# A hybrid SSD and GLA trunk layer: part two begins with the last block's u, held in SBUF

## Chip, cores and metric

The kernel runs on one core of a Trainium2 chip. The metric is the time of one execution on the device, in microseconds; lower is better. The engines are named as in the profile: PE is TensorE (PEld its weight loads), DVE VectorE, ACT ScalarE, POOL GpSimd, SP SyncE, which issues most DMAs.

## What is computed

One layer over 2048 tokens and 16 meta tokens ahead of them, model width 1024, all in float32:

```
u = rmsnorm(h)
z, xbc, dt, q, k, v, g, a_lr, merge_g = split(u @ w_in)
y_ssd = rmsnorm_groups(ssd(conv(xbc), dt) * silu(z))        # 4 groups, state carried along the tokens
y_gla = rmsnorm_heads(gla(q, k, v, a_lr)) * silu(g)         # 4 heads, chunks of 64 tokens
merged = sum over b of sigmoid(merge_g[b]) * (y_b @ w_branch[b])
out = final_rmsnorm(h + merged @ w_out)
```

## The kernel before

Every float32 product is made of three products of split operands: an operand is split into a rounded high part (ACT copies it to fp32r) and the rest (DVE or POOL subtracts), and `accum` (L183-187) issues high by high, high by low and low by high. These are L185, L186 and L187 in the profile.

**Part one** goes over four blocks of 512 tokens (block 0 has the 16 meta tokens besides). `u` of a block is held split in SBUF, in a pool of two tiles, so that `u` of the last block lies there until part one ends; a copy goes to DRAM. In a block come four groups of the SSD branch and four heads of the GLA branch. Each is a projection (u by weights, `ssd_proj` or `gla_proj`), whose generator yields between its pieces, and a scan (`ssd_scan` or `gla_scan`), a generator that `step()` advances by one piece at each of those yields: the scan of a head runs beside the projection of the next. Behind the last head there is no projection left beside which its scan could run. Weights come through a ring of four tiles `whl` (`load_w`, L158-168). In block 0 a weight of 128 x 512 is read from DRAM, split by ACT (L165) and POOL (L166), and its split form, 512 KB, is saved to DRAM (L181); later blocks read that back and split nothing (L161).

The last `gla_scan` has these steps: L688 to L695 on DVE and ACT (decays), L703 on PE, in bank `pc`, L773 and L724 and L790 on PE in bank `pt`, L781 on DVE, which completes an operand from `pt`; then for each chunk L185 to L187 and L801 on PE into `pc`, L802 on DVE (the state), L804 and L806 on ACT (the chunk's output and its square sum, after which `pc` is free); then `rstd`, L811 on ACT, transposes L816 on PE, L817 on DVE, and the store of y (L820, issued by ACT).

**Part two** computes gates, branch products and the output product by a Strassen-Winograd scheme: a product of 2 x 2 tiles takes seven products P1 to P7 of 12 matmuls of 128 x 512 each, instead of eight. A is the weight (a pair n of weight tiles), B the activations of two blocks. P1 and P2 take the first column of B as it lies (`B11`, `B21`), P3 the other; P4 to P7 take sums of B, which are made beside part one and lie in DRAM. Stages come in the order gate0, branch 0 and 1 of blocks 0 and 1, gate1, branch 0 and 1 of blocks 2 and 3, out. In a `Stage`, `load_b` (L898) and `prep_b` (L903 on ACT, L904 on DVE) load and split an operand of B, `load_a` (L910) loads four 256 KB tiles of A of a pair, `sum_a` (L919 to L922 on POOL, four operations) makes A's sums, `prep_a` splits (L928 on ACT, L929 on DVE), `product` issues the matmuls and copies a result that is needed again (L945). A gate is finished by a sum (L965), tanh (L972) and a store (L1104).

PE's and SP's instructions stand in the order in which the code issues them (`manual_schedule`); for ACT, DVE and POOL a scheduler sets the order, except that SP alone is by hand once the loop of stages has begun. The dictionary `between` says what is issued between the steps of the last scan: loads and splits for P1 and P2 of the pairs 0 and 1 of gate0, and P1 and P2 of pair 0; the products of pair 1 follow, moved up among them. `inputs.close()` gives the memory of u and of the weights to these operands. Behind the scan a table `todo` gives each load and split its place (positions in `order`), and `run(i)` issues what is due.

## Time and profile before

| what | value |
|---|---|
| runs shown | 2332.26, 2326.44, 2332.66 us; median 2332.26 |
| profiled execution | 2329.27 us |
| its span | 2327.3 us |
| mean granted TensorE clock | 0.988 |
| busy: PE, DVE, ACT, POOL | 97%, 67%, 51%, 29% of the span |
| DMA | 518.05 MB, mean 223 GB/s |

The page gives busy time of each engine, the span in 40 slices, and groups of instructions with the idle time ahead of them. The timeline lists instructions by start; the brackets at the end of a row give the idle time of the engine just before it and what ended it. Rows marked SPq or ACTq are issues of DMAs on that engine's queue. The windows cut the span into stretches.

### The profile page before, as it was taken

What the parts mean: (1) busy time and instruction counts of PE and PEld (TensorE: products, weight loads), DVE (VectorE), ACT (ScalarE), POOL (GpSimd) and SP (SyncE); (2) the same over time, 40 slices, a digit from 0 to 9 for tenths busy, and PEclk for the clock granted to TensorE, in tenths of its full rate; (3) what the DMA queues carried; (4) which work ended last, traced back from release to release, by engine and by line L of the source; (5) the groups of instructions that cost most, each with busy time, mean ns of one, the idle gap of its engine ahead of it and who ended that gap; (6) DMA issues with size and microseconds to landing.
All of it is one profiled execution on the core that took longest, in us unless ns stands there. A gap on an engine that the chain in (4) does not pass through costs nothing. (4 is left out here: it accounts for less than half of the span.)

```text
span 2327.3 us, 36519 instructions
## 1 busy us (share of the span) xinstructions
PE 2247.1 (97%) x12641; PEld 1956.3 (84%) x12641; DVE 1550.3 (67%) x2895; ACT 1184.8 (51%) x2758; POOL 684.6 (29%) x681
## 2 busy tenths in 40 slices
PE   7899999999999999999999999889999999999998
PEld 7899888888888989898988898768888888888776
DVE  5676766676675666566568555654588954788766
ACT  4666655465544455544465443554554545554443
POOL 3344433122221122212122100037324264324331
PEclk9999999999999999999999999989999999999999
DMA  8766865767785666786677655457577866687743
GB/s 302 230 204 208 292 228 205 223 199 237 244 284 181 214 213 217 255 270 215 194 230 214 206 168 162 145 178 247 186 255 268 305 227 216 231 286 259 243 145 122
DMA packets 301545, 518.05 MB, mean 223 GB/s; under 512 B 27696, under 2 KB 143664, under 8 KB 301360
## 3 DMA queue, kind: packets, MB, share of 16 engines
q1 hardware_dynamic: 200400, 402.84, 53.0%
q10 hardware_dynamic: 100960, 112.88, 14.1%
q8 instruction: 99, 1.62, 0.3%
q14 instruction: 86, 0.70, 0.1%
HBM read 368.42 MB, written 147.19 MB: 222 GB/s over the span
## 5 line engine op out<-in xcount | busy, mean ns | idle before, releaser
L185 PE MATMUL pj<-u,whl 128*128 128x512 f32 (+1 forms) x1184 | 449.0, 379 | 14.6 <-ACT acc L475 6.7
L187 PE MATMUL pj<-u,whl 128*128 128x512 f32 (+1 forms) x1184 | 433.5, 366 | 1.4 <-POOL whl L166 0.8
L186 PE MATMUL pj<-u,whl 128*128 128x512 f32 (+1 forms) x1184 | 432.0, 365 | 0.0
L185 PE MATMUL pj<-whl,u 128*128 128x256 f32 (+1 forms) x992 | 289.0, 291 | 2.4 <-ACT u L298 1.5
L187 PE MATMUL pj<-whl,u 128*128 128x256 f32 (+1 forms) x992 | 282.4, 285 | 1.6 <-DVE u L300 1.6
L186 PE MATMUL pj<-whl,u 128*128 128x256 f32 (+1 forms) x992 | 282.2, 284 | 1.0 <-POOL whl L166 1.0
L185 PEld LDWEIGHTS pj<-u,whl 128*128 128x128 f32 x1184 | 226.8, 192 | 53.7 <-ACT acc L475 7.7
L185 PE MATMUL pj<-b,a 128*128 128x512 f32 x640 | 254.0, 397 | 13.8 <-ACT sn L945 7.6
L187 PEld LDWEIGHTS pj<-u,whl 128*128 128x128 f32 x1184 | 226.0, 191 | 38.0 <-POOL whl L166 1.9
L186 PEld LDWEIGHTS pj<-u,whl 128*128 128x128 f32 x1184 | 227.0, 192 | 33.6
L187 PE MATMUL pj<-b,a 128*128 128x512 f32 x640 | 252.2, 394 | 0.0
L186 PE MATMUL pj<-b,a 128*128 128x512 f32 x640 | 251.0, 392 | 0.0
L185 PEld LDWEIGHTS pj<-whl,u 128*128 128x128 f32 x992 | 189.7, 191 | 4.0 <-ACT u L298 1.8
L187 PEld LDWEIGHTS pj<-whl,u 128*128 128x128 f32 x992 | 189.6, 191 | 2.3 <-DVE u L300 2.3
L80 POOL TENSOR_TENSOR wr<-wr 128x256 f32<-128x256 f32 x80 | 66.3, 829 | 425.0 <-DMA wr<-u 174.7
L186 PEld LDWEIGHTS pj<-whl,u 128*128 128x128 f32 x992 | 189.9, 191 | 1.6 <-POOL whl L166 1.2
L166 POOL TENSOR_TENSOR whl<-wr,whl 128x512 fp32r<-128x512 f32 (+1 forms) x100 | 134.7, 1355 | 187.4 <-ACT whl L165 151.5
L904 DVE TENSOR_TENSOR b<-br,b 128x512 fp32r<-128x512 f32 x196 | 154.9, 808 | 44.7 <-ACT b L903 43.5
L919 POOL TENSOR_TENSOR as<-ar,ar 128x512 f32<-128x512 f32 x40 | 60.0, 1499 | 411.3 <-DMA ar<-in_w_br 197.3
L479 DVE SCALAR_TENSOR_TENSOR acc<-cin,hcw,acc 128x512 f32<-128x512 f32 (+1 forms) x192 | 154.4, 804 | 30.9 <-ACT acc L475 29.8
L929 DVE TENSOR_TENSOR a<-ar,a 128x512 fp32r<-128x512 f32 x160 | 126.3, 797 | 67.2 <-ACT a L928 64.4
L903 ACT ACTIVATE b<-br 128x512 fp32r<-128x512 f32 x196 | 119.4, 626 | 99.0 <-DMA br<-br_t 38.6
(274 smaller groups left out, 5068.8 us busy)
## 6 DMA issues: line engine op xcount, KB each, us to landing
whl<-k_s SPq DMA_DIRECT2D x96, 512.0 KB, 4.5
whl<-k_g SPq DMA_DIRECT2D x96, 512.0 KB, 4.2
whl<-k_v SPq DMA_DIRECT2D x48, 512.0 KB, 3.7
whl<-k_z SPq DMA_DIRECT2D x36, 512.0 KB, 3.8
wr<-in_w_feat SPq DMA_DIRECT2D x64, 256.0 KB, 4.5
k_s<-whl SPq DMA_DIRECT2D x32, 512.0 KB, 3.6
cb<-cumd ACTq DMA_DIRECT2D x64, 256.0 KB, 5.8
y<-gg ACTq DMA_DIRECT2D x64, 256.0 KB, 4.5
```

What stands on the lines that cost most here:

```text
L80: nc.gpsimd.tensor_tensor(o, x, y, op=ALU.subtract)
L166: nc.gpsimd.tensor_tensor(hl[:, 1], raw, hl[:, 0].bitcast(F32), op=ALU.subtract)
L185: nc.tensor.matmul(ps, sh, mh, start=first, stop=False, **kw)
L186: nc.tensor.matmul(ps, sh, ml, start=False, stop=False, **kw)
L187: nc.tensor.matmul(ps, sl, mh, start=False, stop=last, **kw)
L479: nc.vector.scalar_tensor_tensor(acc, cin[:, k:k + tt], hcw[:, ti, k:k + 1], acc, op0=ALU.mult, op1=ALU.add)
L903: nc.scalar.activation(t[:, 0], raw, AF.Copy)
L904: nc.vector.tensor_tensor(t[:, 1], raw, t[:, 0].bitcast(F32), op=ALU.subtract)
L919: nc.gpsimd.tensor_tensor(s1, a21, a22, op=ALU.add)
L929: nc.vector.tensor_tensor(t[:, 1], src, t[:, 0].bitcast(F32), op=ALU.subtract)
```

## The change

Four things are changed; the code's lines move by 5 in `accum` and `load_w`, and more behind.

1. `block_of` makes the last block of a pair the first column of B, so P1 and P2 of gate1 read u of block 3. The stages begin with gate1, then gate0, then the branches. The sums of the branches of blocks 2 and 3, which were made beside gate0 and gate1, are made beside gate1 and gate0.
2. In block 0 `load_w` is called for six weights more, one behind each of the first six heads: those of P1 and P2 of gate1's pairs 0, 1 and 2. They are split and saved like the others.
3. In the last block, from its last head but one on, `early_operands` loads and splits the four B sums of P6 (four loads, four splits) and makes the sums of A for P6 of pairs 0 and 1 (six loads, four POOL operations, two splits), into the tile of u that is free by then.
4. Between the last scan's pieces stand six products, P1 and P2 of the pairs 0, 1, 2, with the six weights (read back from DRAM in split form) and u as it lies in SBUF. Behind the scan's last transposes come the two P6. The loads for the rest of gate1 come behind these, in pools that lie where part one's `first` pool lay; `inputs.close()` follows. Then P7, P5, P3 and P4 of pairs 0 and 1, P1 and P2 of pair 3, and the order as before. A has seven buffers (five and two) in place of six.

```diff
+    def block_of(s, t):
+        return 2 * s + 1 - t
     def braw_u(s):
-        return lambda k, t: u_left[2 * s + t][k]
+        return lambda k, t: u_left[block_of(s, t)][k]
...
+    EARLY = [(n, p) for n in range(3) for p in (1, 2)]
+    last_sums = sums["g", nsb - 1][1][1]
+    b6, s2 = [], {}
+    def gate_w(n, p):
+        return f"m{n}_{p}", w_feat[T_GATE + 2 * n, :, (p - 1) * BLK:p * BLK]
+    def early_operands():
+        room = mk(upool, [P, 2, KT * (META + BLK)], F32R, "u").rearrange("p i f -> p (i f)")
+        tiles = [room[:, j * 1024:(j + 1) * 1024].rearrange("p (i c) -> p i c", i=2) for j in range(6)]
+        b6.extend(tiles[:4])
+        for j in range(0, 4, 2):
+            stage = [mk(wpool, [P, BLK], F32, "wr", bufs=NWR) for _ in range(2)]
+            for i in range(2):
+                nc.sync.dma_start(stage[i], last_sums[j + i][:, 0])
+            yield
+            for i in range(2):
+                split(b6[j + i][:, 0], b6[j + i][:, 1], stage[i])
+            yield
+        for n in range(2):
+            raw = [mk(wpool, [P, BLK], F32, "wr", bufs=NWR)]
+            raw += [mk(wk, [P, META + BLK], F32, "acc")[:, :BLK] for _ in range(2)]
+            for dst, i, j in zip(raw, (1, 1, 0), (0, 1, 0)):
+                nc.sync.dma_start(dst, w_feat[T_GATE + 2 * n + i, :, j * BLK:(j + 1) * BLK])
+            yield
+            nc.gpsimd.tensor_tensor(raw[0], raw[0], raw[1], op=ALU.add)
+            nc.gpsimd.tensor_tensor(raw[0], raw[0], raw[2], op=ALU.subtract)
+            yield
+            s2[n] = tiles[4 + n][:, 0], tiles[4 + n][:, 1]
+            split(*s2[n], raw[0])
...
+            if (b, i) == (nblk - 1, SG + GH - 2):
+                begin(early_operands())
...
+            if b == 0 and i < len(EARLY):
+                load_w(*gate_w(*EARLY[i]))
...
-    inputs.close()
...
-        def product(self, n, p, early=False):
+        def product(self, n, p, early=None, place=None):
             key, pool, tag = {1: ("a", pj, "pj"), 6: ("a",) * 3, 5: ("a",) * 3, 3: ("a",) * 3, 2: ("c", pc, "pc"),
                               7: ("b", pt, "pt"), 4: ("b",) * 3}[p]
             if p in (1, 2, 7):
                 self.ps[n, key] = bank(pool, tag)
             ps = self.ps[n, key]
-            a = self.a[n][p]
...
+            if early is None:
+                a = self.a[n][p]
+                parts = [(a[:, 0, j], a[:, 1, j]) for j in range(4)], [self.b[p, j] for j in range(4)]
+                parts = parts[0], [(t[:, 0], t[:, 1]) for t in parts[1]]
+            else:
+                parts = [tuple(t[:, j * P:(j + 1) * P] for t in early) for j in range(4)], self.early_b(p)
+            for j, (aj, bj) in enumerate(zip(*parts)):
+                accum(ps, aj, bj, p in (1, 2, 7) and j == 0, j == 3, skip_group_check=True)
...
+        def early_b(self, p):
+            if p == 6:
+                return [(t[:, 0], t[:, 1]) for t in b6]
+            return [tuple(t[:, j + 4 * (p - 1), :BLK] for t in next_u[nblk - 1]) for j in range(4)]
...
-    stages = []
+    stages = [gate_stage(s) for s in reversed(range(nsb))]
     for s in range(nsb):
-        stages += [gate_stage(s), branch_stage(s, 0), branch_stage(s, 1)]
+        stages += [branch_stage(s, 0), branch_stage(s, 1)]
...
-    NEARLY = 4
-    order[:NEARLY] = [(stages[0], n, p) for n in range(2) for p in (1, 2)]
+    order = [(stages[0], n, p) for p in PS[3:] for n in range(2)] + [(stages[0], 3, 1), (stages[0], 3, 2)] + order[18:]
+    begins = [max(0, k - 8) for k in begins]
...
-    between = {
-        0: [lambda: st.load_a(0), lambda: b_ops(1, (0, 1))],
-        1: [lambda: b_ops(1, (2, 3)), lambda: st.prep_a(0, 1)],
-        2: [lambda: st.load_a(1), lambda: b_ops(2, (0, 1))],
-        3: [lambda: b_ops(2, (2, 3)), lambda: st.prep_a(0, 2)],
-        4: [lambda: st.product(0, 1, True), lambda: st.prep_a(1, 1)],
-        5: [lambda: st.sum_a(0)],
-        6: [lambda: st.product(0, 2), lambda: st.prep_a(1, 2)],
-        7: [lambda: st.sum_a(1)],
-    }
+    ops = {e: load_w(*gate_w(*e)) for e in EARLY[:4]}
     k = 0
-    while running or begun or k in between:
-        for fn in between.get(k, []):
-            fn()
-        if running or begun:
-            step()
+    while running or begun:
+        step()
+        flush_all()
+        if k in (4, 5):
+            ops[EARLY[k]] = load_w(*gate_w(*EARLY[k]))
+        e = {0: 0, 1: 1, 2: 2, 3: 3, 4: 4, 5: 5}.get(k)
+        if e is not None:
+            place = mk(wk, [P, META + BLK], F32, "acc")[:, :BLK] if EARLY[e][1] == 1 else None
+            st.product(*EARLY[e], ops.pop(EARLY[e]), place)
         k += 1
+    assert not ops
+    flush_all()
+    first.close()
+    bpl.update({p: pool2(f"bops{p}", 4, side="right") for p in (7, 5)})
+    rpl = pool2("raws", 1, side="right")
+    apl = [(pool2("aops", 5, side="right"), 5)] * 5
+    opl, spl = pool2("outs", 1, side="right"), pool2("small", 4, side="right")
+    for n in range(2):
+        st.product(n, 6, s2[n])
+    run(-1)
     ordered.close()
-    first.close()
-    bpl.update({p: pool2(f"bops{p}", 4, side="right") for p in (6, 7, 5, 3, 4)})
-    opl, spl = pool2("outs", 1, side="right"), pool2("small", 4, side="right")
-    bt_raws["all"] = opl, "br", 5
+    inputs.close()
+    bpl.update({p: pool2(f"bops{p}", 4) for p in (3, 4, 1, 2, 6)})
+    apl += [(pool2("aops2", 2), 2)] * 2
```

PE, at the end of the last scan. `pt` behind `cst,ot` are the scan's last transposes (L816 before, L821 after), `pc` ahead of them the last product among the scan's steps, `pj` or `pt` behind them the first one after it. Before:

```order
L185 MATMUL pc_17603<-b_2974_17323,a_17440 128x512
L186 MATMUL pc_17603<-b_2974_17323,a_17440 128x512
L187 MATMUL pc_17603<-b_2974_17323,a_17440 128x512
L816 MATMUL pt_17443<-cst,ot_17341 128x128 x4
L816 MATMUL pt_17449<-cst,ot_17341 128x128 x4
L185 MATMUL pj_17367<-b_3006_17500,a_17512 128x512
L185 MATMUL pj_17575<-b_3006_17500,a_17523 128x512
L186 MATMUL pj_17367<-b_3006_17500,a_17512 128x512
```

And after:

```order
L190 MATMUL pc_17492<-u_11363,whl_17490 128x512
L191 MATMUL pc_17492<-u_11363,whl_17490 128x512
L192 MATMUL pc_17492<-u_11363,whl_17490 128x512
L821 MATMUL pt_17507<-cst,ot_17398 128x128 x4
L821 MATMUL pt_17513<-cst,ot_17398 128x128 x4
L190 MATMUL pj_17278<-u_16199 128x512
L191 MATMUL pj_17278<-u_16199 128x512
L192 MATMUL pj_17278<-u_16199 128x512
```

The last product of the scan reads a weight `whl` and u in place of loaded and split operands `a` and `b`; behind the transposes stands P6 with both operands in the second u tile (`u_16199`), and 24 rows on P7 with loaded operands.

ACT, in the middle of the last scan; `a<-ar` and `b<-br` are splits of operands of part two, the rest are the scan's steps. Before:

```order
L928 ACTIVATE a_17232<-ar_17144 128x512
L691 ACTIVATE sq_17018<-sq_17018 128x64x4
L692 ACTIVATE sq_17018<-sq_17018 128x64x4
L928 ACTIVATE a_17326<-ar_17150 128x512
L903 ACTIVATE b_2924_17154<-br_2923_17152 128x512
L804 ACTIVATE ot_17162<-pc_17164 128x256
L903 ACTIVATE b_2926_17159<-br_2925_17157 128x512
L806 ACTIVATE junk_17174,ssq_17163<-pc_17164 128x256
```

And after:

```order
L696 ACTIVATE sq_17097<-sq_17097 128x64x4
L697 ACTIVATE sq_17097<-sq_17097 128x64x4
L809 ACTIVATE ot_17217<-pc_17219 128x256
L811 ACTIVATE junk_17229,ssq_17218<-pc_17219 128x256
L696 ACTIVATE sq_17247<-sq_17247 128x128x2
L697 ACTIVATE sq_17247<-sq_17247 128x128x2
L809 ACTIVATE ot_17217<-pc_17231 128x256
L811 ACTIVATE junk_17241,ssq_17218<-pc_17231 128x256
```

The splits are gone from between the scan's steps; nothing else stands there in their place.

SP, around the first loads of part two; `k_g` and `k_m` are weights in split form, `in_w_feat` raw weights, `gate_t` sums of B, `u` u in DRAM. Before:

```order
L161 DMA whl_16966<-k_g_0_5132 128x1024
L161 DMA whl_16980<-k_g_1_5151 128x1024
L910 DMA ar_17144<-in_w_feat 128x512
L910 DMA ar_17146<-in_w_feat 128x512
L910 DMA ar_17148<-in_w_feat 128x512
L910 DMA ar_17150<-in_w_feat 128x512
L898 DMA br_2923_17152<-u_0_64 128x512
L898 DMA br_2925_17157<-u_1_65 128x512
```

And after, the six weights and the start of the loads behind the scan:

```order
L166 DMA whl_17209<-k_m_1_936 128x1024
L166 DMA whl_17211<-k_m_2_1607 128x1024
L166 DMA whl_17213<-k_m_1_2254 128x1024
L166 DMA whl_17215<-k_m_2_2895 128x1024
L166 DMA whl_17466<-k_m_1_3506 128x1024
L166 DMA whl_17490<-k_m_2_4081 128x1024
L948 DMA ar_17572<-in_w_feat 128x512
L948 DMA ar_17574<-in_w_feat 128x512
```

Six further `ar` rows follow, then eight `br<-gate_t` rows. In their place before stood the loads of the first weights and of u; there these were issued at the start of the last scan, and after the change the `ar` loads stand behind the two P6.

More of the change, by code (lines that the diff above doesn't have):

```diff
@@ L881, in trunk_kernel @@
               for b in range(nblk)]
+    turn = [0]
     class Stage:
@@ L937, in product @@
             ps = self.ps[n, key]
-            a = self.a[n][p]
-            for j in range(4):
-                bt = self.b[p, j]
-                accum(ps, (a[:, 0, j], a[:, 1, j]), (bt[:, 0], bt[:, 1]), p in (1, 2, 7) and j == 0, j == 3,
-                      skip_group_check=True)
+            if early is None:
[6 more added lines that the diff above has]
+                accum(ps, aj, bj, p in (1, 2, 7) and j == 0, j == 3, skip_group_check=True)
             if p in (1, 6, 5):
-                sn = mk(rpl, [P, 4, P], F32, "as", bufs=6).rearrange("p k c -> p (k c)") if early else mk(opl, [P, BLK], F32, "sn", bufs=6)
+                sn = place if place is not None else mk(opl, [P, BLK], F32, "sn", bufs=6)
                 nc.scalar.activation(sn, ps, AF.Copy)
@@ L1069, in load_sum_a @@
         st.sum_a(n)
+    begun_pairs = set()
     for i, (st, n, p) in enumerate(order):
-        if p == 1 and i >= NEARLY:
-            at(i - LOAD + (n % 2), lambda st=st, n=n: load_sum_a(st, n))
+        if (st, n) not in begun_pairs:
+            begun_pairs.add((st, n))
+            first_at = {0: -1, 1: -0.99, 3: 2, 2: 3} if st is stages[0] else {}
+            at(first_at.get(n, i - LOAD + (n % 2)), lambda st=st, n=n: load_sum_a(st, n))
+    begins_b = {7: -0.98, 5: -0.9, 3: 0.5, 4: 1.8, 1: 3.2, 2: 4.4, 6: 5.6}
     for si, st in enumerate(stages):
-        for q in range(0 if si else 8, 28):
+        for q in range(28):
             p, j = PS[q // 4], q % 4
-            pos = begins[si] - 12 + 0.8 * q if si else -0.99 + 0.2 * (q // 4) if q < 16 else 2 * (q // 4 - 4)
-            at(pos - (4 if si else 0.1), lambda st=st, p=p, j=j: st.load_b(p, j))
+            pos = begins[si] - 12 + 0.8 * q if si else begins_b[p] + (0.3 * j if p not in (7, 5) else 0.001 * j)
+            at(pos - (4 if si else 0.5 if p not in (7, 5) else 0.0005), lambda st=st, p=p, j=j: st.load_b(p, j))
             at(pos, lambda st=st, p=p, j=j: st.prep_b(p, j))
     for i, (st, n, p) in enumerate(order):
-        if i >= NEARLY:
-            at(i - AHEAD if i >= AHEAD + NEARLY else -0.95 + 0.1 * i, lambda st=st, n=n, p=p: st.prep_a(n, p))
+        at(i - AHEAD if i >= AHEAD else -0.95 + 0.01 * i, lambda st=st, n=n, p=p: st.prep_a(n, p))
         if p in DONE:
             at(i - 2, lambda st=st, n=n, p=p: st.fetch(n, *DONE[p]))
-    for key, st in zip(late, (stages[0], stages[-4])):
+    for key, st in zip(late, stages):
         i, end = begins[stages.index(st)] + 9, begins[stages.index(st) + 1] - 16
```

37 lines of the change are left out of this document (17 added, 20 removed).

## Prediction

> **What bounds the kernel now.** I read the page's busy times and its 40 slices first, to see which engine sets the span.
>
> ```profile
> PE 2247.1 (97%) x12641; PEld 1956.3 (84%) x12641; DVE 1550.3 (67%) x2895; ACT 1184.8 (51%) x2758; POOL 684.6 (29%) x681
> ## 2 busy tenths in 40 slices
> PE   7899999999999999999999999889999999999998
> ```
>
> TensorE is busy for 97% of the span. Between the first two slices and the last it dips only in the 26th and 27th (1455 to 1571 us), where part one hands over to part two. The change leaves the matmuls as they are, so it can win only what TensorE loses there, and can lose anywhere that a new wait appears. So I cut that seam into windows of 5 us (start and end, width, busy time and instructions of PE, PEld, DVE, ACT, POOL, then the granted clock, DMA share, GB/s).
>
> ```profile
> 1495.00:1500.00 5.00, 3.76 (x20) 2.59 (x20) 5.00 (x14) 1.92 (x6) 0.00 (x0) 1.00 0.95 306
> 1500.00:1505.00 5.00, 2.60 (x10) 2.31 (x11) 4.42 (x12) 4.04 (x12) 0.00 (x0) 0.64 0.33 108
> 1505.00:1510.00 5.00, 3.96 (x16) 3.08 (x14) 3.40 (x7) 2.76 (x7) 0.00 (x0) 0.68 0.91 313
> 1510.00:1515.00 5.00, 1.85 (x12) 1.48 (x12) 4.23 (x9) 3.34 (x11) 2.22 (x2) 1.00 0.38 111
> 1515.00:1520.00 5.00, 3.22 (x15) 3.17 (x15) 4.43 (x5) 2.81 (x8) 4.92 (x5) 0.50 0.02 6
> 1520.00:1525.00 5.00, 4.83 (x21) 4.01 (x21) 2.28 (x5) 1.50 (x6) 1.45 (x2) 0.81 0.28 105
> ```
>
> This is the first of two holes, the last scan: TensorE is busy for half of it, at half clock for much of that. TensorE's timeline names the waits and shows the second hole, ahead of 1543 (start, duration, line, tiles; in brackets the idle time before it and what ended it).
>
> ```profile
> 1491.04 0.39 PE L185 MATMUL pj<-u,whl 128*128 128x512 f32 x1
> ...
> 1493.77 0.38 PE L790 MATMUL pt<-cst,sq 128*128 128x128 f32 x2
> ...
> 1502.34 2.51 PE L703 MATMUL pc<-sq 128*128 128x128 f32 x8 [2.59 <-ACT junk L806]
> ...
> 1510.50 0.71 PE L703 MATMUL pc<-sq 128*128 128x128 f32 x4 [1.07 <-ACT junk L806]
> ...
> 1516.78 0.66 PE L790 MATMUL pt<-cst,sq 128*128 128x128 f32 x2 [4.42 <-DVE sq L781]
> ...
> 1536.19 1.04 PE L816 MATMUL pt<-cst,ot 128*128 128x128 f32 x8
> 1543.32 1.22 PE L185 MATMUL pj<-b,a 128*128 128x512 f32 x2 [6.10 <-ACT b L903]
> ...
> 1549.04 0.46 PE L185 MATMUL pj<-b,a 128*128 128x512 f32 x1
> ```
>
> ACT's timeline says why the first three last so long: in ACT's program splits of operands stand between the scan's steps, and they wait for a DMA, with the scan behind them.
>
> ```profile
> 1496.57 0.63 ACT L928 ACTIVATE a<-ar 128x512 fp32r<-128x512 f32 x1 [1.09 <-DMA ar<-in_w_feat]
> ...
> 1499.91 0.63 ACT L928 ACTIVATE a<-ar 128x512 fp32r<-128x512 f32 x1 [1.83 <-DMA ar<-in_w_feat]
> 1500.50 0.63 ACT L903 ACTIVATE b<-br 128x512 fp32r<-128x512 f32 x1
> 1501.03 0.37 ACT L804 ACTIVATE ot<-pc 128x256 f32<-128x256 f32 x1
> 1501.30 0.62 ACT L903 ACTIVATE b<-br 128x512 fp32r<-128x512 f32 x1
> 1501.82 0.37 ACT L806 ACTIVATE junk<-pc 128x256 bf16<-128x256 f32 x1
> ```
>
> L804 and L806 free the bank for which L703 waits until 1502.34. That wait began 2.59 earlier, at 1499.75; two splits ahead of L804 and one between it and L806 fill it. DVE shows the like: the split that ends at 1515.98 stands just ahead of L781, for which TensorE waits until 1516.78.
>
> ```profile
> 1515.04 0.94 DVE L904 TENSOR_TENSOR b<-br,b 128x512 fp32r<-128x512 f32 x1 [0.73 <-ACT b L903]
> ```
>
> **Term 1, the last scan: 12 us less.** From 1493.8 to the end of the last transposes (1536.19 + 1.04 = 1537.2) it takes 43.4 us. In it lie four products of 12 matmuls. Twelve 128x512 matmuls at full clock stand between 1491.04 and 1493.77: 2.73 for a product (0.2275 each), so 10.9 for four. The scan's own matmuls at full clock: 64 of 128x256 (the three products of L185 to L187, and L801) at half of that, 7.3, and 38 small ones (L703, L724, L773, L790, L816) at about 0.15 (L816: 1.04 for eight), 5.7, together 13.0. So 43.4 - 10.9 - 13.0 = 19.5 us are lost; of these the half clock is about 4.7 (busy time times what is missing of the clock, over 1500 to 1525), the rest is waits.
>
> In the changed order no operand of part two is loaded raw or split between these pieces. Eight loads of u, eight of weights, eight splits on each of ACT and DVE for B and four for A leave that stretch (splits of the same kind come back later, with the stage in full flow); six 512 KB re-reads of split weights take their place on SP, which need no split. The waits of 2.59 and 1.07 shrink to what L804 and L806 take, about 0.7; of the 4.42, about 1.7 was the L904 and its wait, and the 2.73 of a product now stands in the rest. What is left is 19.5 less the three waits (8.1) and the clock's 4.7, 6.7, and the 0.7: 7.5 lost in place of 19.5, so 12 less. Two more products stand in the scan than before, 5.5 us. The last transposes then end at 1493.8 + 13.0 + 16.4 + 7.5 = 1530.7. At the ends, 3.5 lost would be a gain of 16, and 12.2 lost (the clock's 4.7 stays) a gain of 7.
>
> In this sum the scan runs at full clock. The row at 1510 has clock 1.00 with a 1.07 wait in it, the rows at 1500 and 1505 0.64 and 0.68 after the 2.59. The Trainium skill, page "TensorE: Matmul & The Clock Gate", section "What's actually happening", has the clock halved after an idle window of about 3.4 us and full again after about 3.4 us of sustained work; by it a scan without such a gap keeps its clock, but here a wait of 2.59 among others was enough, and by that row the drop could come back, which is the 4.7 above.
>
> **Term 2, behind the scan: 3.2 us more.** The two P6 come next, 24 x 0.2275 = 5.5, to 1536.2. Then TensorE waits for P7, whose operands now are loaded after the scan, since their tiles lie where the scan's were: the first weight load waits for the last store of a gate tile, and others for the last two y stores.
>
> ```profile
> 1493.96 1.76 SPq L910 DMA_DIRECT2D ar<-in_w_feat  x4
> ```
> ```profile
> 1538.46 1.59 ACTq L820 DMA_DIRECT2D y<-gg  x2
> ```
> ```profile
> y<-gg ACTq DMA_DIRECT2D x64, 256.0 KB, 4.5
> ```
> ```profile
> 1517.08 1.27 POOL L921 TENSOR_TENSOR ar<-ar,ar 128x512 f32<-128x512 f32 x1
> 1518.30 1.75 POOL L922 TENSOR_TENSOR as<-ar,as 128x512 f32<-128x512 f32 x1
> ```
>
> The y stores were issued 2.3 us after the last transposes began (1536.19 to 1538.46); after 1529.7 that makes 1532. A store on a quiet queue I take at 2 us, below the median of 4.5, which is of loaded queues. So SP issues eight weight loads from about 1534.4, 0.44 us each. From the ACT rows the first of such loads landed 2.6 us after its issue (1493.96 to 1496.57) and the fourth 5.95 (1499.91): the fourth lands at 1540.3. POOL makes the sum for pair 0 in three operations, which I take at 1.30 (the rows have 1.27 and 1.75), by 1544.2. ACT and DVE split it, 0.6 and 0.7. P7 starts at about 1545.5. The sums of B stand behind all eight weight loads on SP, and at 0.7 us a load the first lands at about 1543.8, with two splits 1545.1, just ahead. TensorE idles for 9.3 us, where it idled 6.1. The half clock behind it (1543.32 to 1549.04 before) lasts as long again: nothing. The ends: 7 us idle if POOL and the stores are quicker, 14 if the stores take their 4.5 and the second sum, four POOL operations on, is late too.
>
> POOL's chain lies on the path here, beside splits on DVE. At 1.75 in place of 1.30 its three operations would put P7 off by 1.4 us, which lies within the ends above. The Trainium skill, page "GPSIMD Engine Reference", section "8. Key points", says that GpSimd shares its SBUF interfaces with VectorE and that the two contend where DVE reads two inputs from SBUF, which would favour the 1.75; both rows fell beside DVE's splits (the windows at 1515 and 1520), so the trace does not set them apart.
>
> **Term 3, block 0: 1.1 us more.** Six weights more are loaded (256 KB), split on ACT and POOL, and saved (512 KB), one behind each of the first six heads. Each takes a turn in a ring of four tiles that feeds TensorE. Of the waits for such tiles, in the first 460 us, there are only these, and POOL has room:
>
> ```profile
>   POOL whl L166: 1.8, 2
>   ACT whl L165: 1.6, 1
> ```
> ```profile
> L166 POOL TENSOR_TENSOR whl<-wr,whl 128x512 fp32r<-128x512 f32 (+1 forms) x100 | 134.7, 1355 | 187.4 <-ACT whl L165 151.5 <-PE pt L187 12.9 <-issue 9.3
> ```
>
> Three waits, 3.4 us, for some 100 tiles: the ring is mostly ahead. I take one wait more of the mean size, 1.1. The lower end is 0. The upper is the whole turn: TensorE lives 2.73 us on a tile of 12 matmuls, six of them are 16.4. The 4.6 MB more on the queues hide beside the heads.
>
> **The rest: 0.** In the last block ten loads, six splits and four POOL operations are added from the last head but one on; POOL does nothing in the windows before 1510, ACT is busy for half of the span, and the products that use the results come last of all, behind the scan. If DVE's part of it were not hidden, it would cost 6 x 0.94 = 5.6 (the L904 row). The stages' new order and a seventh buffer for A change what each stage loads, not how much.
>
> **Sum.** The profiled execution took 2329.27 us (span 2327.3), 3 below the median of the runs, 2332.26, and between their lowest and highest. 2329.27 - 12 + 3.2 + 1.1 = **2321.6**.
>
> **The rivals.** For the last of them, the page's row of a weight's re-read (KB of one, median us to landing):
>
> ```profile
> whl<-k_g SPq DMA_DIRECT2D x96, 512.0 KB, 4.2
> ```
>
> - *More is won.* The scan's gaps close nearly wholly under six products (3.5 lost, 4 us more won) and P7 comes after 7 us idle (2.3 more): 2315.3. For it: products stand at every place where TensorE waited. Against: DVE is 5.00 and 4.42 busy in the windows at 1495 and 1500, and only part of that is splits. Chance 0.16.
> - *The wait moves.* P7's chain (stores, eight loads, POOL, splits) takes 14 us, and the second pair's sum is late: 4.7 less won, 2326.3; with the clock's 4.7 back as well, 2331. For it: the chain starts only when the scan has ended, while before, weights of both pairs had been loaded during it. Chance 0.18.
> - *Slower: the ring in block 0.* If the six extra turns cost TensorE their 2.73 each, 16.4 in place of 1.1, the time is 2336.9. It decides from 1.5 us a turn on, where it eats the 8.8 of the seam. For it: the DMA engines are nearly full at the start, and every extra load, split and save is in SP's and POOL's order ahead of weights that TensorE will want. Against: the waits of 3.4 us above. Other places where a load comes late in part two, which I did not price, would show the same sign; with them 0.22.
> - *It doesn't do what it says.* The six products wait for their weights (4.2 us to landing, 1.5 over a product's 2.73): 6 x 1.5 is 9 and the seam wins nothing, 2330. Against: the ring lets four be read while the last projection runs. No chance of its own beside the second rival: 0.02.
>
> **How the numbers follow.** The forecast has 0.42. A measurement of this kernel can tell about 0.3%, 7 us, from no change. The forecast lies at 7.7 below, with some 4 either way: 0.25 of it counts as faster, 0.17 as the same. Faster: 0.25 + 0.16 = 0.41. Same: 0.17, 0.16 of the second rival and 0.02, so 0.35. Slower: the third rival and the rest of the second, 0.24. The range goes from 2313 (the first rival and 2 for the spread of runs) to 2337 (the third).
>
> **What would show it.** In the changed trace: no ACT split waits for a DMA between the last projection and the last transposes; these end some 36 to 38 us after the projection; P6 follows with no gap; then one wait of 9 us on TensorE, ended by a split of a sum, with POOL's sums just ahead of it; and no waits for weight tiles in block 0 beyond 5 us. If TensorE's wait ahead of P7 is over 13 us, or waits for weights grow to 10, I am wrong; if the scan still has a row with clock 0.6, term 1 is.

## The result, and the profile after

The change made the kernel slower: 2341.66 us (median of six runs, 2336.1 to 2346.2) against 2330.91 of six runs of the kernel before, a ratio of 1.0048, 95% interval 1.0028 to 1.0068. The forecast was 2321.6 with a range of 2313 to 2337, so time and sign were both missed. The profiled execution of the changed kernel took 2336.1 us, the lowest of its six, 7 more than that of before; so its trace shows somewhat less than the difference of the medians. Each run below is set against runs of the kernel before that were taken with it; their medians lie between 2330.91 and 2332.42, so where two changed versions are compared the ratios are given besides the medians.

The page of the changed kernel:

```profile
PE 2251.8 (96%) x12641; PEld 1949.7 (84%) x12641; DVE 1556.3 (67%) x2893; ACT 1184.6 (51%) x2762; POOL 696.6 (30%) x691
## 2 busy tenths in 40 slices
PE   7899999999999999999999999979999999999998
```

TensorE's busy time grew by 4.7 us with the same 12641 matmuls: that is the first sign that not only waits changed. The slices dip in the 27th alone. The same 5 us windows of the seam, after (the columns are those of the prediction):

```profile
1495.00:1500.00 5.00, 3.98 (x23) 3.38 (x24) 5.00 (x15) 3.32 (x11) 0.00 (x0) 1.00 0.00 0
1500.00:1505.00 5.00, 4.92 (x30) 3.97 (x29) 1.55 (x4) 2.02 (x7) 0.00 (x0) 1.00 0.36 107
1505.00:1510.00 5.00, 5.00 (x26) 4.11 (x25) 3.32 (x8) 2.85 (x9) 1.46 (x1) 1.00 0.16 51
1510.00:1515.00 5.00, 4.92 (x32) 4.06 (x30) 2.80 (x6) 1.86 (x5) 0.00 (x0) 1.00 0.55 212
...
1535.00:1540.00 5.00, 0.00 (x0) 0.00 (x0) 0.18 (x1) 0.65 (x2) 4.62 (x4) 0.62 1.03 348
1540.00:1545.00 5.00, 3.12 (x6) 1.71 (x7) 5.00 (x4) 3.13 (x5) 4.92 (x4) 0.50 0.49 184
1545.00:1550.00 5.00, 3.80 (x12) 1.88 (x10) 5.00 (x7) 3.74 (x7) 2.08 (x2) 0.85 0.61 179
...
1570.00:1575.00 5.00, 2.37 (x6) 1.06 (x6) 4.10 (x5) 3.78 (x8) 4.92 (x4) 0.88 0.62 201
```

The first hole is closed: the scan runs at clock 1.00 and nearly without idle time. The second is there as forecast, and it goes on longer than forecast: from 1540 to 1548 TensorE does few matmuls although it has begun (at half clock at first, as behind the hole before the change), and at 1570 there is a third hole. TensorE's timeline at the second:

```profile
1531.78 0.39 PE L192 MATMUL pj<-u 128*128 128x512 f32 x1
1540.66 0.79 PE L190 MATMUL pt<-b,a 128*128 128x512 f32 x1 [8.49 <-ACT b L941]
1542.63 0.79 PE L191 MATMUL pt<-b,a 128*128 128x512 f32 x1 [1.18 <-DVE b L942]
```

The wait of 8.49 was forecast at 9.3. The second wait was not forecast. DVE's line L942 (the low half of a split of B), first in the stretch of P7, then in the next 15 us (count, and shortest, median and longest duration in ns), and POOL's L959:

```profile
L942 DVE TENSOR_TENSOR b<-br,b x4: 1755/1759/1764, 1540.8 to 1545.9; 128x512 fp32r<-128x512 f32 x4
...
L942 DVE TENSOR_TENSOR b<-br,b x12: 675/678/1762, 1545.9 to 1559.1; 128x512 fp32r<-128x512 f32 x12
```
```profile
L959 POOL TENSOR_TENSOR ar<-ar,ar x2: 1262/1490/1717, 1537.9 to 1543.7; 128x512 f32<-128x512 f32 x2
```

While POOL makes the sums, DVE's split takes 1.76 us; after POOL has ended (1547), 0.68. POOL's own operation goes from 1.26 to 1.72 once DVE has begun. The Trainium skill's rule on the SBUF interfaces that GpSimd shares with VectorE ("GPSIMD Engine Reference", section "8. Key points") is borne out; I priced it for POOL alone (1.4 us at most), while DVE pays more: these four splits take 4.3 us longer, and P7 is fed by them. Over the whole trace, the 154 splits of L942 with no POOL operation beside them took 0.674 to 0.695 us, and the 28 that lay wholly beside POOL's took 1.49 in the median.

Matched by the number of matmuls done, the changed kernel was 2.6 us ahead at the last projection's end (1491.2 against 1493.8), 5.7 at about 1600, 3.5 at 1730, 2 behind at 1930, 7.3 behind at 2085, 14.2 behind at 2200, and 7.0 behind at the end. The seam thus gave 3.1, in place of 8.8, and then 13 were lost in the stretch from 1600 to the end, which the prediction had put at nothing. What TensorE waited for from 1640 us to the end, before and after:

```profile
PE pj L185 <- ACT sn L945: 6.2, 5, 3.6
```
```profile
PE pj L190 <- ACT sn L989: 8.7, 10, 2.2
PE pj L192 <- DVE a L969: 3.0, 3, 1.4
```

That is 11.7 us against 6.2. Up to 2200 us it is 11.7 against 0.7; the rest of the waits of before lie behind 2200, where the changed kernel has none, and there it makes up 7 us of its lag. And where nothing waits, a matmul itself is slower. Here is the product P2 of two pairs (24 matmuls) in the middle of a stage, first and last row, of before and of after:

```profile
1735.13 0.39 PE L185 MATMUL pc<-b,a 128*128 128x512 f32 x1
...
1740.35 0.39 PE L187 MATMUL pc<-b,a 128*128 128x512 f32 x1
```
```profile
1731.69 0.40 PE L190 MATMUL pc<-b,a 128*128 128x512 f32 x1
...
1737.06 0.39 PE L192 MATMUL pc<-b,a 128*128 128x512 f32 x1
```

23 steps take 5.21 us before (unrounded) and 5.37 after: 0.2267 and 0.2335 each. Taken over all products between 1720 and 2000 us and leaving waits out, the mean step is 0.2288 before and 0.2311 after. Part two has some 3380 such matmuls, so this is 7.8 us. Sorted by operand, over all from 1600 us on, the step after the change is 0.2333 where A lies high in SBUF and B low, 0.2297 the other way round, and 0.2269 or 0.2285 where both lie high or both low. Before, all A tiles were low; the change put five of seven high. For the stretch from 1600 to the end the 5.5 us of waits and some 7 of slower steps (0.0023 x 3080) come to the 13 that were lost.

So two theories stood for the loss behind the seam. **The place** (later: the alignment) of A and B makes matmuls slower. **The seventh buffer of A** changes ACT's order, which makes the waits. The rivals were that the stages' new order makes the waits, that what runs beside TensorE makes the matmuls slow, and that block 0's six weights cost more than priced.

### The profile page after: what moved, and what is told of

Read it like the earlier page. It is cut to its first block, busy times and chain, and to the rows that moved or that the text cites. A ratio compares the mean times of both kernels' runs of the same rounds, so it can differ in the third digit from the quotient of the medians.

```text
span 2334.3 us, 36553 instructions
## 1 busy us (share of the span) xinstructions
PE 2251.8 (96%) x12641; PEld 1949.7 (84%) x12641; DVE 1556.3 (67%) x2893; ACT 1184.6 (51%) x2762; POOL 696.6 (30%) x691
## 4 chain that ended last, share of the span: by engine, by line
PE 42%; DMA 12%; DVE 7%; issue 4%; ACT 4%; POOL 2%; SPq 2%; ACTq 0%; POOLq 0%; DVEq 0%
PE pj L190 9%; PE pj L192 9%; PE pj L191 9%; DMA br<-br_t 2%; DVE b L942 2%; PE pt L191 1%; PE pt L192 1%; DVE a L969 1%; PE pt L190 1%; DMA acc<-in_xmt 1%; PE pc L190 1%; PE pc L192 1%; PE pc L191 1%; PE pc L708 1%; DMA io<-g 1%
## 5 line engine op out<-in xcount | busy, mean ns | idle before, releaser
L190 PE MATMUL pj<-b,a 128*128 128x512 f32 x620 | 242.9, 396 | 10.5 <-ACT sn L989 9.1
L192 PE MATMUL pj<-b,a 128*128 128x512 f32 x620 | 243.9, 394 | 3.0 <-DVE a L969 3.0
L191 PE MATMUL pj<-b,a 128*128 128x512 f32 x620 | 244.1, 394 | 1.0 <-DVE b L942 1.0
L171 POOL TENSOR_TENSOR whl<-wr,whl 128x512 fp32r<-128x512 f32 (+1 forms) x106 | 142.9, 1356 | 184.3 <-ACT whl L170 146.0
L942 DVE TENSOR_TENSOR b<-br,b 128x512 fp32r<-128x512 f32 x196 | 157.7, 828 | 59.2 <-ACT b L941 56.0
L969 DVE TENSOR_TENSOR a<-ar,a 128x512 fp32r<-128x512 f32 x154 | 133.0, 878 | 75.6 <-ACT a L968 74.9
```

The source lines that it names most:

```text
L171: nc.gpsimd.tensor_tensor(hl[:, 1], raw, hl[:, 0].bitcast(F32), op=ALU.subtract)
L190: nc.tensor.matmul(ps, sh, mh, start=first, stop=False, **kw)
L191: nc.tensor.matmul(ps, sh, ml, start=False, stop=False, **kw)
L192: nc.tensor.matmul(ps, sl, mh, start=False, stop=last, **kw)
L942: nc.vector.tensor_tensor(t[:, 1], raw, t[:, 0].bitcast(F32), op=ALU.subtract)
L969: nc.vector.tensor_tensor(t[:, 1], src, t[:, 0].bitcast(F32), op=ALU.subtract)
```

## The experiments

**A low, six buffers.** In this kernel `inputs` is closed ahead of the first loads, and A's tiles take the memory of the weights:

```diff
-    bpl.update({p: pool2(f"bops{p}", 4, side="right") for p in (7, 5)})
+    bpl.update({p: pool2(f"bops{p}", 4, side="right") for p in (7, 5, 6)})
-    apl = [(pool2("aops", 5, side="right"), 5)] * 5
...
-    run(-1)
-    ordered.close()
     inputs.close()
-    bpl.update({p: pool2(f"bops{p}", 4) for p in (3, 4, 1, 2, 6)})
-    apl += [(pool2("aops2", 2), 2)] * 2
+    bpl.update({p: pool2(f"bops{p}", 4) for p in (3, 4, 1, 2)})
+    apl = [(pool2("aops", 6), 6)]
+    run(-1)
+    ordered.close()
```

> The changed kernel with A's split tiles (six of them) and the B tiles of P3, P4, P1, P2 in the low part of SBUF, A where it lay before the change, and the tiles of P6 high. Nothing else differs. Theory of the place: a matmul with its stationary operand (A) high and its moving operand (B) low takes 0.2333 us, other pairs 0.2267 to 0.2296, which is some 8 us over part two; and the seventh buffer of A changed ACT's order, with some 7 us of waits at the ends of stages. Both are gone here: mean of a dense matmul at 0.229 again, waits of TensorE between 1640 and 2260 us down from 14 to 7, time 12 to 15 us below the changed kernel, about 2327, a little faster than before. Rival (the stages' order and the late loads cost the time): rows and waits stay, time stays within 3 us of the changed kernel, 2341.

Measured: 2327.55 us (median of 12) against 2332.42 of before, ratio 0.9979 (0.9964 to 0.9993). The mean step between 1720 and 2000 us is 0.2280. Both losses are gone, and the kernel is 4.9 us (1.6 to 8.4) faster than before. Not all of that is the change as planned: the step is shorter than that of before as well (0.0008 x 3380 is 2.7 us). And the edit does more than its expectation says. With the tiles in other places the eight weight loads are issued from 1511.7 us on in place of 1530.8, TensorE waits 5.4 us ahead of P7 in place of 8.5, and the seam gives 7.5 in place of 3.1. Which part weighs what, this run doesn't say.

**Six buffers alone.**

```diff
-    apl += [(pool2("aops2", 2), 2)] * 2
+    apl += [(pool2("aops2", 1), 1)]
```

> The changed kernel with six buffers for A in place of seven (five high, one low). Theory: ACT's order at the ends of stages is that of before again, and 4 to 7 us of TensorE's waits go; matmuls stay at 0.231 or a little slower (five of six A tiles are high), so the time comes 3 to 7 us below the changed kernel, about 2336. Rival (the waits come from the stages' order): waits as in the changed kernel, time 2341 to 2344.

Measured: 2336.98, ratio 1.0018 (1.0003 to 1.0034), 4.7 below the changed kernel by the medians and 7.0 by the ratios (1.0018 against 1.0048). Between 1640 and 2200 us the trace has no wait of TensorE, and behind 2200 waits of 3.7 us in all, where the changed kernel had 11.7 before 2200 and none behind; the steps with A high and B low stay at 0.2333. The stages' order is that of the changed kernel, so the rival for the waits falls. How a buffer makes waits can be read from ACT's timeline at the end of gate0, first of before, then with six buffers, then of after (with TensorE's wait); `b<-br` are splits for the next stage, `sn<-pj` is the copy of P5 for which TensorE's P3 waits:

```profile
1677.27 0.60 ACT L945 ACTIVATE sn<-pj 128x512 f32<-128x512 f32 x1 [2.11 <-PE pj L187]
...
1682.47 0.63 ACT L903 ACTIVATE b<-br 128x512 fp32r<-128x512 f32 x1 [3.22 <-DMA br<-br_t]
```
```profile
1832.82 0.60 ACT L989 ACTIVATE sn<-pj 128x512 f32<-128x512 f32 x1 [1.57 <-PE pj L192]
...
1837.30 0.63 ACT L941 ACTIVATE b<-br 128x512 fp32r<-128x512 f32 x1 [2.49 <-DMA br<-br_t]
```
```profile
1833.42 0.63 ACT L941 ACTIVATE b<-br 128x512 fp32r<-128x512 f32 x1 [6.54 <-DMA br<-br_t]
1834.22 0.63 ACT L941 ACTIVATE b<-br 128x512 fp32r<-128x512 f32 x1 [0.17 <-DMA br<-br_t]
1834.76 0.58 ACT L989 ACTIVATE sn<-pj 128x512 f32<-128x512 f32 x1
```
```profile
1835.39 0.50 PE L190 MATMUL pj<-b,a 128*128 128x512 f32 x1 [1.23 <-ACT sn L989]
```

Before and with six buffers, the copy stands ahead of the splits that wait for a DMA; after, two of them stand ahead of it, and ACT idles 6.5 us for their DMA; TensorE waits the last 1.23 us for the bank that ACT should copy. ACT's order is not written in the code: the scheduler sets it, and with seven buffers it puts B's splits ahead of the copy. Why it does so, no run shows.

**P7's A made early.** `early_operands` makes a11 - a21 of pairs 0 and 1 as well, into the two tiles of u that were left, and the loads of P7's B go ahead of the weights':

```diff
-        tiles = [... for j in range(6)]
+        tiles = [... for j in range(8)]
...
+            for i in range(2):
+                nc.sync.dma_start(raw[i], w_feat[T_GATE + 2 * n + i, :, :BLK])
...
+            nc.gpsimd.tensor_tensor(raw[1], raw[0], raw[1], op=ALU.subtract)
...
+            split(tiles[6 + n][:, 0], tiles[6 + n][:, 1], raw[1])
...
+        st.product(n, 7)
     ordered.close()
```

> The changed kernel with P7's A operands of pairs 0 and 1 made in the last block as well (two loads, one POOL operation, one split for each), and the loads of P7's B ahead of the weights' behind the scan. Theory of the seam: DVE's splits took 1.76 us in place of 0.68 because POOL's sums ran beside them, and P7 waited for weights, sums and these splits; here the splits of P7's B run before POOL's sums and at 0.7 us, TensorE waits 3 to 4 us in place of 8.6, and 5 to 8 us are won: about 2335. Rival (the wait only moves on to P5, whose sums POOL makes): 0 to 3 us won.

Measured: 2342.2, ratio 1.0035 (1.0021 to 1.005), which can't be told from the changed kernel's 1.0048 (1.0028 to 1.0068); a gain of 5 to 8 us is not there. In its trace the seam alone (from the last projection to 1600) gives 5.2 in place of 3.1. TensorE's waits ahead of and within P7 fall to 1.4 us; P5 then waits 3.4 for its operands and a product in `pj` at 1578 to 1582 waits 3.8. The wait moves on, as the rival has it.

**Matmuls alone, by place.** A kernel of products only, after loads and splits are done (`STAT` names seven of the `NSLOT` = 50 places):

```diff
+        for a in STAT:
+            for b in range(NSLOT):
...
+                for j in range(4):
+                    sh, sl = [slots[a][:, i, j * P:(j + 1) * P] for i in range(2)]
+                    mh, ml = slots[b][:, 0], slots[b][:, 1]
+                    nc.tensor.matmul(p, sh, mh, start=j == 0, stop=False)
+                    nc.tensor.matmul(p, sh, ml, start=False, stop=False)
+                    nc.tensor.matmul(p, sl, mh, start=False, stop=j == 3)
```

> Matmuls alone: products of 12 with A in one of seven places (16.5, 57.5, 98.4, 118.9, 139.4, 180.4, 217.2 KB from the start of a partition, in thousands of bytes) and B in each of the other 49 places of 4 KB; nothing of the reference is computed. Theory: the time from start to start depends on the two places: 0.226 to 0.228 where both lie low or both high, 0.233 with A high and B low, 0.229 with A low and B high, with a bound between 106 and 147 thousand bytes. Rival (what differs in part two is what runs beside TensorE): one time, 0.226 to 0.228, for all places.

Measured: 0.2270 us (the median of a product's steps) for every one of the 343 pairs but the first, which fell in the slow clock. My theory of the place fell with it. But all tiles of this kernel lay in steps of 4096 bytes from one start, and those of the changed kernel did not: by the addresses of the built programs, its low tiles begin at remainder 160 of 256 bytes, its high ones at 224. So the theory became one of alignment.

**Matmuls alone, by alignment.** The same products with A and B at eight steps of 32 bytes each:

```diff
+    for an in ("a_low", "a_high"):
+        for bn in ("b_low", "b_high"):
+            for ao in range(0, 64, 8):
+                for bo in range(0, 64, 8):
+                    at, bt = T[an][:, ao:ao + 1024], T[bn][:, bo:bo + 1024]
```

> Matmuls alone again, since the last such run showed one time for all places of 4 KB steps: there every tile began at the same remainder of 128 bytes. Now A and B each begin at eight steps of 32 bytes, in four pairs of low and high places; nothing of the reference is computed. Theory of the alignment: the pair of remainders decides: 0.227 where A and B have the same remainder of 128 bytes or of 64, 0.229 or 0.233 (16 cycles of 2.4 GHz more for one in three or for all) with A at remainder 96 and B at 32 or the reverse, whatever the place. Rival (it is the place together with other engines' work): one time, 0.227, for all.

Two of its products, first and last of 12 matmuls, with nothing else running: A and B both at remainder 160 of 256, then A at 224 and B at 160 (both low in SBUF):

```profile
37.65 0.40 PE L71 MATMUL p_a_low_b_low<-b_low,a_low 128*128 128x512 f32 x1
...
40.15 0.39 PE L73 MATMUL p_a_low_b_low<-b_low,a_low 128*128 128x512 f32 x1
...
82.25 0.39 PE L71 MATMUL p_a_low_b_low<-b_low,a_low 128*128 128x512 f32 x1
...
84.81 0.39 PE L73 MATMUL p_a_low_b_low<-b_low,a_low 128*128 128x512 f32 x1
```

11 steps take 2.50 us in the one and 2.56 in the other. The means of a step, in us, for the remainders that the kernels have:

```
A at, B at (of 256)   A low, B low   A low, B high   A high, B low   A high, B high
160, 160                 0.2273          0.2272          0.2272          0.2272
224, 224                 0.2272          0.2289          0.2273          0.2289
160, 224                 0.2296          0.2297          0.2297          0.2297
224, 160                 0.2325          0.2330          0.2326          0.2330
```

These are nearly the numbers of part two, without any other engine at work and nearly without regard to the place: the rival falls. Over all remainders the steps go from 0.2272 to 0.2346 (without the first two products, which fell in the slow clock). Equal remainders of 256 give 0.2272 to 0.2290; B 64 bytes further than A, as with 160 and 224, gives 0.2285 to 0.2299 in all 32 such products; all other pairs give 0.2325 to 0.2346. My guess that a remainder of 128 decides was too coarse: A at 32 and B at 160 took 0.2329.

**64 bytes of padding, in the changed kernel and in the kernel before.** One line behind `first.close()`, so that every tile of A and B begins at remainder 160 of 256 (32 of 128):

```diff
+    mk(pool2("pad", 1, side="right"), [P, 16], F32, "pad")
```

> The changed kernel with 64 unused bytes above its high pools, so that all tiles of A and B begin at remainder 32 of 128 bytes; A stays high, B of P3, P4, P1, P2, P6 low. Theory of the alignment: mean of a dense matmul 0.227 in place of 0.2313, some 3300 of them, 10 to 14 us less than the changed kernel: about 2329. Rival (the place, high against low, or what runs beside): 0.2333 with A high and B low as before, time 2341.

> The kernel before with the same 64 unused bytes. Theory of the alignment: the matmuls of P3 to P7, whose B lies high and A low, go from 0.2290 to 0.2268, 5 of 7 products of 3400 matmuls: 4 to 6 us less than before, 2326. Rival: no change.

Measured: the changed kernel 2334.15, ratio 1.0012 (0.9997 to 1.0026); the kernel before 2324.37 against 2331.32, ratio 0.9975 (0.9958 to 0.9991). The mean step falls to 0.2268 and 0.2267. The windows from 1700 to 1820 of the changed kernel, without and with the 64 bytes, each without a wait:

```profile
1700.00:1820.00 120.00, 120.00 (x521) 97.53 (x520) 56.48 (x74) 55.55 (x98) 56.93 (x54) 1.00 0.59 195
```
```profile
1700.00:1820.00 120.00, 120.00 (x531) 99.38 (x530) 58.18 (x75) 57.24 (x102) 60.25 (x56) 1.00 0.61 203
```

531 matmuls in place of 521 in the same time, with TensorE busy throughout in both: a busy engine is not one at its peak. For the kernel before the whole gain shows (0.0021 x 3380 = 7.1 us, and 7.0 are measured, with an interval of 2 to 10). The changed kernel should win 14.5 by its steps and wins 7.5 by the medians, 8.4 by the ratios. Its waits from 1640 us on are what they were (11.8 for 11.7). Its trace is of the slowest of its executions: it lies 13 us behind the unpadded one's already at the last projection, in code that the padding doesn't touch, and behind 1600 it wins 10.1. Where the rest of the 14.5 goes, the runs don't show.

**Block 0's weights alone, in the kernel before.**

```diff
+            if b == 0 and i < 6:
+                load_w(f"m{i // 2}_{1 + i % 2}", w_feat[T_GATE + 2 * (i // 2), :, i % 2 * BLK:(i % 2 + 1) * BLK])
```

> The kernel before with one thing of the change alone: the six weights are loaded, split and saved in block 0, and nothing uses them. My third term gave 1.1 us, its ends 0 and 16.4, and the rival that the ring in block 0 makes the change slower 16. From the runs with A low I now expect 3 to 5 us: 2335 to 2337.

Measured: 2335.16, ratio 1.0019 (1.0004 to 1.0033): 3.8 us, with an interval of 0.9 to 7.7. TensorE's longest wait for a weight's high part in the first 460 us went from 1.6 to this:

```profile
PE pj L185 <- ACT whl L165: 2.2, 1, 2.2
```

So waits for the ring's tiles are not what costs it, and its trace was 2.9 us behind that of before at 337 us and 6.3 at 693. But single traces can't divide 3.8 us: at the last projection the changed kernel's trace is 2.7 ahead of before's, and that of the same kernel with the 64 bytes 10.3 behind. What the 3.8 consist of stays open.

**The seventh buffer, at one alignment.** The 64 bytes and six buffers:

```diff
-    apl += [(pool2("aops2", 2), 2)] * 2
+    apl += [(pool2("aops2", 1), 1)]
+    mk(pool2("pad", 1, side="right"), [P, 16], F32, "pad")
```

> The changed kernel with the 64 bytes and six buffers of A (five high, one low). At equal remainders the place of a tile no longer matters, so against the run with the 64 bytes alone (2334) this shows the seventh buffer by itself. Theory of ACT's order: 4 to 7 us less, 2327 to 2330. Rival (the waits at the ends of stages are the stages' order): 2333 to 2335.

Measured: 2325.08, ratio 0.9972 (0.9959 to 0.9985), 9.1 below the run with the 64 bytes alone (9.3 by the ratios), more than I had put. TensorE's waits for the copies between 1640 and 2200 us, with seven buffers and with six:

```profile
PE pj L190 <- ACT sn L989: 9.1, 8, 2.1
```
```profile
PE pj L190 <- ACT sn L989: 2.5, 4, 0.9
```

With six there are 5.5 more behind 2200, with seven none, and seven have 2.7 more for other splits; so up to the end the waits are 11.8 and 8.0. They explain some 4 of the 9; in the traces the stretch behind 1600 differs by 7.7.

**A low with the 64 bytes.** The first experiment's edit and the padding.

> The run with A low and six buffers (2327.6), with the 64 bytes besides. Theory of the alignment: P5, P6 and P7, whose B lies high, go from 0.229 to 0.227, three sevenths of 3400 matmuls, 3 to 4.5 us less: 2323 to 2325. What then stands beside the kernel before with the same 64 bytes (2324.4) is the change alone: what the seam gives, 7, less what block 0 takes, 4, so 2321 to 2325. Rival (the change is worth nothing without the side effects): no difference from 2324.4 beyond 1.

Measured: 2323.13 (median of 7), ratio 0.9969 (0.9957 to 0.9981). It is the fastest version that was run, below both kernels; but the kernel before with the same 64 bytes has 0.9975, and the intervals lie over each other. So, freed of alignment and buffers, the change moves nothing that these runs can tell.

**P7 early, and the weights in block 1.** Two more steps on the last kernel: the third experiment's edit, and then `load_w` for the six weights with `b == 1`, each raw load issued a piece ahead and saved at once.

```diff
-            if b == 0 and i < len(EARLY):
+            if b == 1 and i < len(EARLY):
                 load_w(*gate_w(*EARLY[i]))
+                save(0)
```

> The last run, and P7's A operands of pairs 0 and 1 made in the last block, P7 issued with the P6 and its B loaded first. In the changed kernel that won some 2 us of the seam (TensorE's wait ahead of P7 went, P5 waited in its place). Expected 1 to 4 us less than the last run, 2320 to 2323. Rival: nothing, as the wait moves to P5.

> The last run, with the six weights loaded, split and saved in block 1 in place of block 0, where the other weights only are read back. Theory: the 3.8 us that the six weights cost in block 0 come from queues and a ring that are full there; block 1 hides them: 2 to 4 us less than the last run, about 2318. Rival (the price is a turn of the ring wherever they stand, or SP's wait for the split ahead of the save costs as much): the same time or more.

Measured: 2332.22, ratio 1.0004 (0.9991 to 1.0017), and 2334.18, ratio 1.0009 (0.9997 to 1.0021): 9 and 11 us worse than the kernel that they started from. What TensorE waited for from 1490 to 1600 us, in that kernel and in the one with P7 early:

```profile
PE pt L190 <- ACT b L941: 5.1, 1, 5.1
```
```profile
PE pj L190 <- ACT b L950: 5.7, 3, 4.6
PE pj L191 <- DVE b L951: 2.9, 3, 2.1
PE pt L190 <- ACT b L950: 1.2, 1, 1.2
```

P7 (in `pt`) waits 1.2 in place of 5.1; P5 (in `pj`) waits 5.1 in its turn, since its B comes behind eight weight loads, and the rest of the `pj` rows is a product at 1581 to 1585. All waits of this stretch together are 15.1 against 12.7, so the wait moves, as the first rival has it, and the seam gets worse (it gives 2.9 in place of 6.6). That is 3.7 of the 10.7 us between the two traces. Another 3.6 are there at the last projection; but 3.7 are there at 200 us already, where both kernels do the same, so they are no price of the last block's extra work. The 3.4 behind 1600 stay unexplained. With the weights in block 1 the time is 2 us longer than with them in block 0, within the intervals: block 1 doesn't hide them, as the second rival has it. Whether the price is a turn in the ring or a wait of SP, these runs don't show.

## Why the prediction was wrong

- **The last scan, 12 us less: right, and a little small.** From the last projection's end to the end of P6 (1491.2 to 1532.2) it took 41.0 us, where the prediction has 1493.8 to 1536.2, 42.4. ACT's splits are gone from the scan, and no window of it has a clock below 1.00; the drop that the trace had made me keep as an end did not come. By the Trainium skill's rule ("TensorE: Matmul & The Clock Gate", section "What's actually happening") a scan without a long idle gap keeps its clock; the trace agrees, for the longest wait in it is 0.6 us.
- **Behind the scan, 3.2 more: the wait right (8.5 for 9.3), the stretch behind it not.** The mis-sized term is DVE's split: 0.7 in my chain, 1.76 measured beside POOL. P7 took 7.8 us from its first to its last step (1540.66 to 1548.48); 1.7 of these are waits for such splits, and the half clock, which had been put at nothing more than before, makes most of the rest, as it did there (5.7 us, 1543.32 to 1549.04). The same contention is there at the hole at 1570, when the next pairs' sums were due: three splits of B took 1.68 each beside POOL, and the clock fell again (0.88 and 0.78). From P7's first step to 1600 TensorE waits 5.5 us, where the kernel before waits 1.0 behind its hole. Of the 8.8 that the two terms were to give, the trace has 3.1.
- **Block 0, 1.1 more: the direction right, the size not.** 3.8 measured (0.9 to 7.7). The rival that named the ring at 16.4 was wrong in size, and the waits for the ring's tiles didn't grow by more than 0.6.
- **"The rest: 0" failed.** The step reads: "The stages' new order and a seventh buffer for A change what each stage loads, not how much." What each stage loads was not the matter, and with six buffers the new order of the stages made no more waits than there were (3.7 us from 1640 on, 6.2 before). The seventh buffer moved ACT's order, which cost 4.7 us by the medians as the kernel stands (7.0 by the ratios) and 9.1 at equal alignment. The pools' new places moved the remainders at which A and B begin, and a matmul's step with them, 0.2288 to 0.2311, some 8 us. The nearest that the prediction came to this is its third rival's remark, "Other places where a load comes late in part two, which I did not price": it is late loads of B that ACT waits for ahead of the copy.
- **The sum.** Changed kernel against the one with 64 bytes and six buffers: 2341.66 to 2325.08, 16.6. The kernel before against itself with 64 bytes: 7.0. So 9.6 of the 10.75 that the change lost are these two side effects, and what is left of the change itself, about 1 us, lies within the intervals. By their sizes the seam's gain (3.1 in the trace) and block 0's price (3.8) would cancel; no run shows them against each other. Apart the two side effects are 4.7 and 7.5 by the medians, 7.0 and 8.4 by the ratios, and together 16.6; with intervals of some 4 us on each, whether they simply add can't be told.
- **The forecast's method.** The terms were sought in the seam since TensorE idled there. 770 us of a full engine lay behind it, in which 1% is 8 us, and it was passed over because the number of matmuls had not changed. Every sign that the prediction had named for itself came true, or nearly (no split between the scan's steps, the transposes 35.5 us after the projection, P6 without a gap, one wait of 8.5 ahead of P7, small waits for weights): all of them lay in the seam and in block 0, and none behind.

What stays open: which part of a matmul or of its weight load pays for unequal remainders, through which waits block 0's weights cost 3.8 us, and why the scheduler orders ACT otherwise with seven buffers.

## What to carry to other kernels

When a change moves pools, compare the start addresses of matmul operands before and after, and measure a dense product's step in both; a busy share of 100% hides a difference of 3% (0.2267 and 0.2333 here). When it changes a number of buffers, look at the order that the scheduler then gives to the engine that feeds and drains TensorE, above all for a copy that now stands behind an instruction waiting for a DMA. Put a price on work that is moved beside another engine's work in the durations of both engines.

## What the hardware showed

- A 128x512 fp32r matmul with its weight load takes 0.2272 to 0.2346 us from start to start, by the remainders of 256 bytes at which the stationary and the moving operand begin in SBUF (3072 matmuls alone, at full clock, from which the table above is taken); 64 bytes of padding made the kernel before faster by 0.25% (0.09 to 0.42).
- A DVE subtraction of two SBUF tiles of 128x512 takes 0.68 us alone and 1.76 beside a POOL operation on two SBUF tiles, whose own time goes from 1.26 to 1.72.
- After an idle time of 8.49 us TensorE's clock was 0.50 from 1540 to 1545.
